# Seven products for more pairs of weight blocks, and two kinds of addition moved from VectorE to adding DMAs

## The chip, the cores and the metric

The kernel runs on one core of a Trainium2 chip. The metric is device time in microseconds: a median of runs, and beside it the time of one profiled execution, from which all rows of the trace come.

## What is computed

A causal decoder trunk of two layers on 256 tokens of width 2048, in float32. Each layer is a token mixer and then an MLP, each behind an RMSNorm, all added into one residual stream:

```python
h = rms_norm(x, mix_norm_g[i]);  x = x + mixer_i(h)        # layer 0: forgetting attention, layer 1: dilated windows
h = rms_norm(x, mlp_norm_g[i])
a = jax.nn.relu(h @ w_up)                                   # 2048 -> 8192
x = x + (a * a) @ w_down                                    # 8192 -> 2048
```

The two MLPs hold the change. In each, `w_up` is 2048 x 8192 and `w_down` is 8192 x 2048.

## The kernel before

**Units and pairs.** A matrix product is cut into units of 512 output columns. A unit walks over its contracted dimension in eight *pairs*: a pair is 256 rows by 512 columns of weights, 512 KB, loaded by SyncE's queue (SP) into a buffer `raw` (`loaded`, L335). Float32 precision is kept by splitting each operand into a high and a low part: ScalarE (ACT) casts `raw` to `hi` (`cut`, L342), VectorE (DVE) subtracts it to get `lo` (L348), and TensorE (PE) multiplies high by high, high by low and low by high.

**Three forms of a pair.** `whole` (L386 to L388) does two chunks of 128 rows, two halves of the tokens and three part products: 12 matmuls of 512 columns. `parts` (L413 to L438) treats the pair as a 2 x 2 block product and does it by seven block products and not eight: 7 x 3 = 21 matmuls of 256 columns. For that it needs sums of token blocks (`sigma`, made once per norm) and sums of weight blocks, made anew for each pair: one DVE addition of 512 columns (L413), two of 256 (L418, L420), and two cuts, one of 768 columns of the weights themselves and one of 1024 columns of the sums. It takes two buffers `raw` (one for the sums), two `hi` and two `lo`; a whole pair takes one of each. `quarters` (L407) is the whole form inside a unit that has `parts` pairs; its 12 matmuls go to the same banks of PSUM.

**The MLP.** It is done in four periods of 2048 hidden columns: `b` = 0 to 3. A period has four up units (`n` = 0 to 3) and, in the period after it, four down units that read their result. From period 1 on, up unit `n` is interleaved with down unit `n` of the period before, pair by pair, by the string `UU_D`; I call these 16 pairs a *round*. There are 12 rounds in each MLP, 24 in all. In period 0 only up units run: the first two share their pairs out as 6, 6, 2, 2, then the third, then the fourth. The table `HALVED[b][n]` says which pairs of an up unit go by `parts`: five of eight in all 24 up units of periods 1 to 3, none in period 0.

**The end of an up unit** (`up_end`): ACT copies four banks to SBUF (L968), DVE combines them by five additions (L973 to L986), ACT applies the ReLU (L991), DVE transposes in blocks (L994), four DMAs and one back take it through DRAM (`through_dram`), ACT squares (L1002) into a buffer `tr`, ACT casts the high part (L1007) and DVE subtracts the low part (L1009) into `aT`, which the down units read. The end of a down unit (`add_to_x`, L527) is one DVE addition of 1024 columns from PSUM into the residual stream.

**What sets the order.** All operations are entered in a plan (`Plan`) with an engine, an estimated time and the buffers they read and write. Buffers come in rings: an item waits until the former user of its slot is done. The plan is run through with the estimates, and the instructions are issued in the order of starts that comes out. The estimates (`on_act`, `on_dve`, `moved`, `gap`) thus shape only the order. Each engine works its own instructions strictly in this order, SP's queue of DMAs too: where the first waits for a buffer, those behind it wait as well. In the MLPs there are 7 `raw` (6 and one of the phase), 5 `hi`, 5 `lo`, and 4 `tr`.

Of the kernel before, what the change touches and what calls it, by code (L numbers as in the profile page):

```python
# [13 lines left out]
ALU = mybir.AluOpType  # L14
# [3 lines left out]
P = 128  # L18
D = 2048
S = 256  # L20
NT = S // P
NC = 512
# [13 lines left out]
PERIODS = DFF // D  # L36
# [52 lines left out]
class Plan:  # L89

    HANDOFF = 0.25
    LANDING = 2.1
    BACKLOG = 2.0
    FIRST = 14.0
# [40 lines left out]
    def gap(self, a, b):  # L137
        if a.eng == "dma":
            return self.LANDING
        if a.eng is None:  # L140
            return 0.0
        if a.eng == b.eng:
            return 0.0 if a.eng == "pe" else 0.06
        return self.HANDOFF

    def order(self, rounds=3):
        for ring in self.rings:
# [81 lines left out]
def trunk(ctx: ExitStack, tc, x, fox_w_in, fox_b_f, fox_q_gain, fox_k_gain, fox_w_out, dil_w_in,  # L229
          dil_q_gain, dil_k_gain, dil_w_out, mix_norm_g, mlp_norm_g, mlp_w_up, mlp_w_down, out):  # L230
    nc = tc.nc
    plan = Plan(["fox", "mlp0", "dil", "mlp1"])
    add = plan.add
    T = {}

    def v(item):
        return T[item.slot if isinstance(item, Item) else item]

    def r(item):
        return v(item).bitcast(F32R)  # L240
# [18 lines left out]
    N_RAW = 6  # L259
    N_HI = 4  # L260
    N_LO = 4
    N_Z = 1
    N_C = 1
    raw_ring = ring("raw", N_RAW, 2 * NC)
# [4 lines left out]
    blocks_ring = Ring(plan, [f"blocks{i}" for i in range(4)])  # L269
    rings = {}  # L270
    for ph in ("mlp0", "mlp1"):
        rings[ph] = dict(sigma=ring("sigma", 4, 2 * 4 * 2 * P, ph), tr=ring("tr", 4, NT * NC, ph),
                         z=ring("z", N_Z, 6 * S, ph), c=ring("c", N_C, NC, ph))
    for ph, n_sets, heads in (("fox", 1, 4), ("dil", 3, 2)):
        rings[ph] = dict(
            s=ring("s", 4, 3 * P, ph), w=ring("w", 4 if ph == "fox" else 3, NT * NC, ph),
# [3 lines left out]
            ph=ring("ph", 2, S, ph), pl=ring("pl", 2, S, ph), pw=ring("pw", 2, P, ph))  # L280
# [163 lines left out]
    def through_dram(turned, into, size=NT * NC):  # L444
        blocks = blocks_ring.take()
        for i in range(4):
            def go(i=i):
                nc.sync.dma_start(v(blocks)[:, :, :, i, :].rearrange("t j c x -> c t j x"),
                                  v(turned)[32 * i:32 * i + 32, 0:size].rearrange("p (t j x) -> p t j x", t=NT, j=4))
            add("dma", 0.45, go, reads=[turned], writes=[(blocks, i)])  # L450
# [24 lines left out]
    def x_keys(n):  # L475
        return [(f"x{n}", t) for t in range(NT)]
# [41 lines left out]
            reads=[room, (sigma, 0)], writes=[(sigma, 1)])  # L518


    def add_to_x(n, then=None):
        def end(banks):
            pair = banks[0].slot[0]

            def go():
                at = v(f"x{n}").rearrange("p (t h n) -> p t h n", t=NT, h=2)
                nc.vector.tensor_add(at, at, v(pair).rearrange("p (t n h) -> p t h n", t=NT, h=2))  # L527
# [413 lines left out]
    out_proj(oT, fox_w_out[0], then1)  # L941


    def up_end(l, phase, source, halved):
        own = rings[phase]

        def end(banks):
            z, turned = own["z"].take(), own["tr"].take()
# [51 lines left out]
            for t in range(NT):  # L1000
# [5 lines left out]
            source.items.append(a)  # L1006
            add("act", on_act(2 * NC), lambda: nc.scalar.copy(r(a)[:, 0:2 * NC], v(turned)), reads=[(turned, t) for t in range(NT)],  # L1007
                writes=[(a, b, 0) for b in range(4)])
            add("dve", on_dve(2 * NC), lambda: nc.vector.tensor_sub(r(a)[:, 2 * NC:], v(turned), v(a)[:, 0:2 * NC]),  # L1009
                reads=[*((turned, t) for t in range(NT)), *((a, b, 0) for b in range(4))], writes=[(a, b, 1) for b in range(4)])  # L1010
        return end

    AC, BE = ("A0", "A1", "C0", "C1"), ("B0", "B1")
    UU_D = "UUDUDUDUDUDUDUDD"

    def mlp(l, layer, phase, source, sigmas, then, last=None):
        for weights, name, n in ((raw_ring, "raw", MORE[0]), (hi_ring, "hi", MORE[1]), (lo_ring, "lo", MORE[2])):
            slots = [f"{phase}_{name}{i}" for i in range(n)]
            in_phase[phase].update({s: 2 * NC for s in slots})
            weights.more(slots, phase)  # L1020
        downs = []
        turn = 0
        for b in range(PERIODS):
            a = Source()
            ups = []
            for n in range(4):
                halved = HALVED[b][n]
                banks = AC if halved else ("A0", "A1") if b or n % 2 == 0 else ("B0", "B1")
                ups.append(Unit(source, mlp_w_up[layer], 0, [(b * D + n * NC, NC)], banks,
                                up_end(l, phase, a, halved), halved, sigmas))  # L1030
            if b == 0:
                paired(ups[0], ups[1])
                ups[2].blocks(NP)
                ups[3].blocks(NP)
            else:
                for u, d in zip(ups, downs):
                    for c in UU_D:
                        (u if c == "U" else d).block()
            downs = []
            for n in range(NX):  # L1040
                banks = ("E0", "E1") if turn % 2 == 0 else ("B0", "B1")
                turn += 1
                end = add_to_x(n, then if b == PERIODS - 1 else None)
# [217 lines left out]
```

## Time and profile before

| | |
|---|---|
| median of 3 runs | 2120.92 us (2120.85 to 2121.04) |
| profiled execution | 2121.22 us; its span from first to last instruction 2119.5 us |
| DVE, ACT, POOL busy | 1669.8, 1266.0, 57.8 us |
| HBM read, written | 455.26, 35.65 MB |
| the 12 rounds of the first MLP | 460.5 to 943.4 us after the span's start |
| the 12 rounds of the second MLP | 1549.0 to 2031.9 us |

A row of the table of groups reads: line, engine, operation, output<-inputs, shape, count, then busy time, mean duration of one in ns, then idle time of the engine just before them and what ended it. PE's matmuls overlap in the records, so their pace is read from the starts in the timeline and not from their durations.

### The profile page before, as it was taken

The page shows a single profiled execution, that of the slowest core. Times are in us where ns is not written, and L with a number is a line of the kernel's source. Part 1 is how long each engine was busy: PE and PEld are TensorE (multiplying, and loading weights), DVE is VectorE, ACT ScalarE, POOL GpSimd, SP SyncE. Part 2 cuts the span into 40 slices and gives each one's busy share as a digit, 9 for nine tenths or more (in the row PEclk, how much of TensorE's full clock was granted, in tenths as well). Part 3 has the DMA queues.
Part 4 walks back from the last instruction along what each step waited for, and adds up shares of the span by engine and source line. Part 5 has one row for each costly group of instructions (what it writes and reads, how often), then busy time and mean ns, then how long its engine had stood idle before and what let it go on. Part 6 is the DMA issues. An engine that isn't in the chain of part 4 may idle for free.

```text
span 2119.5 us, 30432 instructions
## 1 busy us (share of the span) xinstructions
PE 2109.8 (100%) x11285; PEld 1888.0 (89%) x11285; DVE 1669.8 (79%) x2092; ACT 1266.0 (60%) x1640; POOL 57.8 (3%) x51
## 2 busy tenths in 40 slices
PE   9999999999999999999999999999999999999999
PEld 7888888889999999998888888888899999999988
DVE  6777777678899899886787777777678898898874
ACT  5555556566666666666555555556666666666652
POOL 1011000000000000000010000000000000000000
PEclk9999999999999999999999999999999999999999
DMA  7777668777767777777786776768767777777773
GB/s 247 233 221 199 212 217 262 240 243 238 228 225 242 241 225 237 245 257 260 227 259 200 235 223 207 249 203 285 237 223 232 249 228 230 248 229 228 248 259 129
DMA packets 336133, 492.93 MB, mean 233 GB/s; under 512 B 21928, under 2 KB 137712, under 8 KB 335984
## 3 DMA queue, kind: packets, MB, share of 16 engines
q1 hardware_dynamic: 335712, 490.86, 72.9%
q8 instruction: 88, 1.44, 0.3%
q14 instruction: 61, 0.50, 0.1%
q10 hardware_dynamic: 272, 0.13, 0.0%
HBM read 455.26 MB, written 35.65 MB: 232 GB/s over the span
## 4 chain that ended last, share of the span: by engine, by line
PE 99%; DMA 0%; SPq 0%; DVE 0%; issue 0%; ACT 0%
PE bank_B L386 11%; PE bank_B L388 11%; PE bank_B L387 11%; PE bank_C L407 9%; PE bank_A L386 7%; PE bank_A L388 7%; PE bank_A L387 7%; PE bank_E L386 7%; PE bank_E L388 7%; PE bank_E L387 7%; PE bank_A L437 3%; PE bank_A L438 3%; PE bank_A L436 3%; PE bank_C L437 2%; PE bank_C L438 2%; PE bank_C L436 2%
## 5 line engine op out<-in xcount | busy, mean ns | idle before, releaser
L342 ACT CAST hi<-raw 128x1024 fp32r<-128x1024 f32 (+1 forms) x720 | 736.0, 1026 | 585.0 <-PE bank_B L388 171.1
L348 DVE TENSOR_TENSOR lo<-raw,hi 128x1024 fp32r<-128x1024 f32 (+1 forms) x720 | 854.7, 1193 | 277.1 <-ACT hi L342 261.7
L386 PE MATMUL bank_A<-hi,hT 128*128 128x512 f32 x552 | 212.0, 384 | 0.0
L388 PE MATMUL bank_A<-hi,hT 128*128 128x512 f32 x552 | 210.3, 381 | 0.0
L387 PE MATMUL bank_A<-lo,hT 128*128 128x512 f32 x552 | 210.2, 381 | 0.0
L386 PE MATMUL bank_B<-hi,aT 128*128 128x512 f32 x520 | 197.5, 380 | 0.5 <-ACT aT L646 0.5
L388 PE MATMUL bank_B<-hi,aT 128*128 128x512 f32 x520 | 197.1, 379 | 0.0
L387 PE MATMUL bank_B<-lo,aT 128*128 128x512 f32 x520 | 197.1, 379 | 0.0
L386 PE MATMUL bank_B<-hi,hT 128*128 128x512 f32 x480 | 183.7, 383 | 0.0
L387 PE MATMUL bank_B<-lo,hT 128*128 128x512 f32 x480 | 181.9, 379 | 0.0
L388 PE MATMUL bank_B<-hi,hT 128*128 128x512 f32 x480 | 181.9, 379 | 0.0
L386 PE MATMUL bank_E<-hi,aT 128*128 128x512 f32 x472 | 179.0, 379 | 0.0
L387 PE MATMUL bank_E<-lo,aT 128*128 128x512 f32 x472 | 178.9, 379 | 0.0
L388 PE MATMUL bank_E<-hi,aT 128*128 128x512 f32 x472 | 178.9, 379 | 0.0
L342 ACT CAST mlp_hi<-raw 128x1024 fp32r<-128x1024 f32 (+1 forms) x108 | 109.7, 1016 | 90.1 <-PE bank_E L388 27.0
L348 DVE TENSOR_TENSOR mlp_lo<-raw,mlp_hi 128x1024 fp32r<-128x1024 f32 (+1 forms) x108 | 127.0, 1176 | 27.7 <-ACT mlp_hi L342 24.1
L407 PE MATMUL bank_C<-hi,hT 128*128 128x512 f32 x430 | 138.5, 379 | 0.0
L388 PEld LDWEIGHTS bank_A<-hi,hT 128*128 128x128 f32 x552 | 104.9, 190 | 15.4 <-DVE hT L711 0.5
L386 PEld LDWEIGHTS bank_A<-hi,hT 128*128 128x128 f32 x552 | 105.1, 190 | 14.0
L387 PEld LDWEIGHTS bank_A<-lo,hT 128*128 128x128 f32 x552 | 105.0, 190 | 14.1
L388 PEld LDWEIGHTS bank_B<-hi,aT 128*128 128x128 f32 x520 | 98.3, 189 | 14.1 <-DVE aT L647 0.2
L386 PEld LDWEIGHTS bank_B<-hi,aT 128*128 128x128 f32 x520 | 98.4, 189 | 13.3 <-ACT aT L646 0.7
(360 smaller groups left out, 4391.7 us busy)
## 6 DMA issues: line engine op xcount, KB each, us to landing
raw<-in_mlp_w_up_dram SPq DMA_DIRECT2D x222, 512.0 KB, 4.5
raw<-in_mlp_w_down_dram SPq DMA_DIRECT2D x222, 512.0 KB, 4.8
raw<-in_fox_w_in_dram SPq DMA_DIRECT2D x96, 512.0 KB, 4.6
raw<-in_dil_w_in_dram SPq DMA_DIRECT2D x192, 256.0 KB, 3.1
blocks<-mlp_tr SPq DMA_DIRECT2D x176, 128.0 KB, 3.6
mlp_z<-blocks SPq DMA_DIRECT2D x44, 512.0 KB, 5.4
mlp_raw<-in_mlp_w_up_dram SPq DMA_DIRECT2D x34, 512.0 KB, 4.5
mlp_raw<-in_mlp_w_down_dram SPq DMA_DIRECT2D x34, 512.0 KB, 4.6
```

The source lines that it names most:

```text
L342: add("act", on_act(n), lambda: nc.scalar.copy(r(hi)[:, 0:n], v(src)[:, at:at + n]), reads=keys, writes=[hi])
L348: add("dve", on_dve(n), lambda: nc.vector.tensor_sub(r(lo)[:, 0:n], v(src)[:, at:at + n], v(hi)[:, 0:n]), reads=[*keys, hi], writes=[lo])
L386: nc.tensor.matmul(acc, a, h, start=first and i == 0, stop=False)
L387: nc.tensor.matmul(acc, a, l, start=False, stop=False)
L388: nc.tensor.matmul(acc, b, h, start=False, stop=last and i == 1)
L407: nc.tensor.matmul(to, m, w, start=False, stop=False)
L436: nc.tensor.matmul(acc, a(0), w(0, at), start=first and edge & 1 == 1, stop=False)
L437: nc.tensor.matmul(acc, a(0), w(1, at), start=False, stop=False)
L438: nc.tensor.matmul(acc, a(1), w(0, at), start=False, stop=last and edge & 2 == 2)
```

## The change

Up pairs by seven products go from 120 to 178: seven of eight in 23 of the 24 up units of periods 1 to 3, six in the other, and six of eight in the third up unit of period 0 of each MLP. The string of a round changes from `UUDUDUDUDUDUDUDD` to `UUUDDUUDDUUDUDDD`.

In periods 0 to 2 of each MLP the end of a down unit no longer adds on DVE: ACT copies its two banks into a new buffer `sums` (two copies of 512 columns) and a DMA issued by GpSimd (POOL) adds this into `x`; these are the 24 residual additions. For the first three up units of each period ACT writes, beside the high part, its negative into the low half of `aT`, and a DMA issued by POOL adds the full value `turned` to that, which leaves the low part; these are the 24 low parts (3 x 4 x 2). The fourth up unit of each period keeps the DVE subtraction.

Buffers: `tr` 4 to 3, one `sums` is new; the phase's own `raw`, `hi`, `lo` go from 1, 1, 1 to 0, 2, 1, so that there are 6, 6 and 5. Up units of period 0 that are not halved use `sums` in the place of `z`. The estimates of the plan change as well.

```diff
-MORE = (1, 1, 1)
-HALVED = [[(), (), (), ()], [FIVE] * 4, [FIVE] * 4, [FIVE] * 4]
+MORE = (0, 2, 1)
+BY_DMA = True
+LOW_BY_DMA = True
+HALVED = [[(), (), (0, 3, 4, 5, 6, 7), ()],
+          [(0, 1, 3, 4, 5, 6, 7), (0, 1, 3, 4, 5, 6, 7), (0, 1, 3, 4, 5, 6, 7), (0, 1, 3, 4, 5, 6, 7)],
+          [(0, 1, 3, 4, 5, 6, 7), (0, 1, 3, 4, 5, 6, 7), (0, 1, 3, 5, 6, 7), (0, 1, 3, 4, 5, 6, 7)],
+          [(0, 1, 3, 4, 5, 6, 7), (0, 1, 3, 4, 5, 6, 7), (0, 1, 3, 4, 5, 6, 7), (0, 1, 3, 4, 5, 6, 7)]]
 def on_act(n, accum=False):
-    return 0.24 + 0.00083 * n + (0.19 if accum else 0)
+    return 0.12 + 0.00083 * n + (0.19 if accum else 0)
 def on_dve(n, inputs=2):
-    return 0.17 + (0.00104 if inputs == 2 else 0.00054) * n
+    return 0.085 + (0.00104 if inputs == 2 else 0.00054) * n
 def moved(kb):
-    return kb / 380.0
+    return kb / 335.0
...
+    def added(to, of, reads, writes, us):
+        add("pool", 1.2, lambda: nc.gpsimd.dma_start(to(), of(), accum_op=ALU.add), reads=[*reads, *writes])
+        add("dma", us, None, reads=reads, writes=writes)
...
+            if room is not None:
+                sums = room.take()
+                for t in range(NT):
+                    def go(t=t):
+                        nc.scalar.copy(halves(v(sums)[:, t * NC:(t + 1) * NC], S), by_column(v(banks[t]), S))
+                    add("act", on_act(NC), go, reads=[banks[t]], writes=[(sums, t)])
+                added(lambda: v(f"x{n}"), lambda: v(sums), [(sums, t) for t in range(NT)], x_keys(n), 2.55)
+                return
...
-            add("dve", on_dve(2 * NC), lambda: nc.vector.tensor_sub(r(a)[:, 2 * NC:], v(turned), v(a)[:, 0:2 * NC]),
...
+            if by_dma:
+                add("act", on_act(2 * NC), lambda: nc.scalar.mul(r(a)[:, 2 * NC:], v(turned), -1.0), reads=whole, writes=low)
+                added(lambda: v(a)[:, 2 * NC:], lambda: v(turned), whole, low, 2.55)
...
-    UU_D = "UUDUDUDUDUDUDUDD"
+    UU_D = "UUUDDUUDDUUDUDDD"
```

More of the change, by code (lines that the diff above doesn't have):

```diff
@@ L142, in gap @@
         if a.eng == b.eng:
-            return 0.0 if a.eng == "pe" else 0.06
-        return self.HANDOFF
+            return 0.0 if a.eng == "pe" else 0.12
+        return 0.3 if a.eng == "pe" else self.HANDOFF
     def order(self, rounds=3):
@@ L261, in trunk @@
     N_LO = 4
+    N_TR = 3
     N_Z = 1
@@ L271, in trunk @@
     for ph in ("mlp0", "mlp1"):
[L272 to L273 removed]
+        rings[ph] = dict(sigma=ring("sigma", 4, 2 * 4 * 2 * P, ph), tr=ring("tr", N_TR, NT * NC, ph),
+                         z=ring("z", N_Z, 6 * S, ph), c=ring("c", N_C, NC, ph), sums=ring("sums", 1, NT * NC, ph))
     for ph, n_sets, heads in (("fox", 1, 4), ("dil", 3, 2)):
@@ L941, in trunk, with up_end @@
     out_proj(oT, fox_w_out[0], then1)
-    def up_end(l, phase, source, halved):
+    def up_end(l, phase, source, halved, by_dma, room):
         own = rings[phase]
         def end(banks):
-            z, turned = own["z"].take(), own["tr"].take()
+            z, turned = own[room].take(), own["tr"].take()
             by = lambda t: v(f"rstd{l}")[:, t:t + 1]
@@ L1008, in end @@
                 writes=[(a, b, 0) for b in range(4)])
-            add("dve", on_dve(2 * NC), lambda: nc.vector.tensor_sub(r(a)[:, 2 * NC:], v(turned), v(a)[:, 0:2 * NC]),
-                reads=[*((turned, t) for t in range(NT)), *((a, b, 0) for b in range(4))], writes=[(a, b, 1) for b in range(4)])
-        return end
-    AC, BE = ("A0", "A1", "C0", "C1"), ("B0", "B1")
-    UU_D = "UUDUDUDUDUDUDUDD"
+            whole = [(turned, t) for t in range(NT)]
+            low = [(a, b, 1) for b in range(4)]
+            if by_dma:
+                add("act", on_act(2 * NC), lambda: nc.scalar.mul(r(a)[:, 2 * NC:], v(turned), -1.0), reads=whole, writes=low)
+                added(lambda: v(a)[:, 2 * NC:], lambda: v(turned), whole, low, 2.55)
+            else:
+                add("dve", on_dve(2 * NC), lambda: nc.vector.tensor_sub(r(a)[:, 2 * NC:], v(turned), v(a)[:, 0:2 * NC]),
+                    reads=[*whole, *((a, b, 0) for b in range(4))], writes=low)
+        return end
+    AC, BE = ("A0", "A1", "C0", "C1"), ("B0", "B1", "E0", "E1")
+    UU_D = "UUUDDUUDDUUDUDDD"
     def mlp(l, layer, phase, source, sigmas, then, last=None):
@@ L1027, in mlp @@
                 halved = HALVED[b][n]
-                banks = AC if halved else ("A0", "A1") if b or n % 2 == 0 else ("B0", "B1")
+                banks = (AC if halved else AC[:2]) if b or n % 2 == 0 else BE if halved else BE[:2]
                 ups.append(Unit(source, mlp_w_up[layer], 0, [(b * D + n * NC, NC)], banks,
-                                up_end(l, phase, a, halved), halved, sigmas))
+                                up_end(l, phase, a, halved, LOW_BY_DMA and n < 3, "z" if b or halved else "sums"), halved, sigmas))
             if b == 0:
@@ L1042, in mlp @@
                 turn += 1
-                end = add_to_x(n, then if b == PERIODS - 1 else None)
+                end = add_to_x(n, then) if b == PERIODS - 1 else add_to_x(n, None, rings[phase]["sums"] if BY_DMA else None)
                 downs.append(Unit(a, mlp_w_down[layer], b * D, [(n * NC, NC)], banks, end, adding=ADDING if b < PERIODS - 1 else ()))
```

6 lines of the change are left out of this document (3 added, 3 removed).

## The prediction

> **What bounds the kernel now.** I read the page first (busy times, clock, the chain that ended last), then PE's waits, PE's timeline, and then, for the rounds alone, the busy times of a window and the waits of DVE.
>
> ```profile
> PE 2109.8 (100%) x11285; PEld 1888.0 (89%) x11285; DVE 1669.8 (79%) x2092; ACT 1266.0 (60%) x1640; POOL 57.8 (3%) x51
> PE 99%; DMA 0%; SPq 0%; DVE 0%; issue 0%; ACT 0%
> PEclk9999999999999999999999999999999999999999
> ```
>
> PE is the bound: the chain of work that ended last lies on it for 99% of the span, at the full granted clock. A busy PE alone would prove little, so I looked for its waits:
>
> ```profile
> PE bank_E L701 <- DMA x<-in_x_dram: 2.1, 2, 1.7
> PE bank_C L659 <- POOL ident masks.py:199: 1.7, 1, 1.7
> PE bank_E L670 <- DMA fox_s<-in_mix_norm_g_dram: 1.3, 1, 1.3
> PE bank_B L1191 <- DVE x L1206: 0.8, 1, 0.8
> PE bank_B L386 <- ACT aT L646: 0.5, 1, 0.5
> ```
>
> That is the whole list (what for, what ended it, total us, times, longest): 6.4 us, at the start, at the end and once before an output projection, nothing in the MLPs. So PE time saved in the rounds comes off the total, as long as nothing else grows past PE there. How much time a pair takes is read from the starts:
>
> ```profile
> 601.13 0.38 PE L386 MATMUL bank_B<-hi,aT 128*128 128x512 f32 x1
> 603.72 0.27 PE L436 MATMUL bank_A<-hi,hT 128*128 128x256 f32 x1
> 606.07 0.38 PE L386 MATMUL bank_B<-hi,aT 128*128 128x512 f32 x1
> ```
>
> From 601.13 to 603.72 lie the 12 matmuls of a whole pair, 2.59 us; from 603.72 to 606.07 the 21 of a pair by seven products, 2.35 us. The rounds of the first MLP check this:
>
> ```profile
> 460.50:943.40 482.90, 482.90 (x2859) 440.73 (x2858) 425.93 (x518) 309.34 (x361) 0.00 (x0) 1.00 0.74 237
> ```
>
> (Window, its length, then busy us of PE, weight loads, DVE, ACT, POOL with their counts; clock, DMA share, GB/s.) A round lasts 482.9 / 12 = 40.24 us. It has 5 pairs of the short form and 11 of the long one; with 2.592 for the long one (12 x 0.216) the short one is (40.24 - 28.51) / 5 = 2.346. The gain per pair is 0.246 us.
>
> **The change: PE.** 58 pairs more (46 in the rounds, 6 in period 0 of each MLP) x 0.246 = 14.3 us. Two more units are split into two forms, which costs nothing in columns. A new round lasts 40.24 - 14.3 x 46 / 58 / 24 = 39.77 us on PE alone.
>
> **DVE.** Here is the price. The rows by shape, and starts that follow one another:
>
> ```profile
> L348 DVE TENSOR_TENSOR lo<-raw,hi 128x1024 fp32r<-128x1024 f32 x642 | 780.8, 1222 | 260.8 <-ACT hi L342 245.7 <-DMA mlp_z<-blocks 2.7 <-DMA raw<-in_mlp_w_down_dram 2.0
> L348 DVE TENSOR_TENSOR lo<-raw,hi 128x768 fp32r<-128x768 f32 x78 | 74.4, 954 | 16.4 <-ACT hi L342 16.0
> L413 DVE TENSOR_TENSOR raw<-raw 128x512 f32<-128x512 f32 x72 | 49.6, 689 | 32.7 <-DMA raw<-in_mlp_w_up_dram 32.3
> L418 DVE TENSOR_TENSOR raw<-raw,raw 128x256 f32<-128x256 f32 x72 | 30.2, 419 | 0.6
> L1009 DVE TENSOR_TENSOR aT<-mlp_tr,aT 128x1024 fp32r<-128x1024 f32 x32 | 39.0, 1217 | 7.6 <-ACT aT L1007 7.3
> L527 DVE TENSOR_TENSOR x<-x,bank_B 128x1024 f32<-128x1024 f32 x19 | 23.1, 1217 | 2.9 <-PE bank_B L388 2.9
> L994 DVE STREAM_TRANSPOSE mlp_tr<-mlp_z 128x1024 f32<-128x1024 f32 x32 | 39.6, 1239 | 3.9 <-ACT mlp_z L953 3.3 <-ACT mlp_z L991 0.7
> L973 DVE TENSOR_TENSOR mlp_z<-mlp_z,mlp_c 128x512 f32<-128x512 f32 x24 | 16.4, 684 | 0.3 <-ACT mlp_z L968 0.3
> L974 DVE TENSOR_TENSOR mlp_z<-mlp_z 128x256 f32<-128x256 f32 x24 | 10.2, 425 | 0.8
> ```
>
> ```profile
> 652.44 0.69 DVE L413 TENSOR_TENSOR raw<-raw 128x512 f32<-128x512 f32 x1
> 653.04 1.22 DVE L348 TENSOR_TENSOR lo<-raw,hi 128x1024 fp32r<-128x1024 f32 x1
> 654.18 0.41 DVE L418 TENSOR_TENSOR raw<-raw,raw 128x256 f32<-128x256 f32 x1
> ...
> 655.12 0.96 DVE L348 TENSOR_TENSOR lo<-raw,hi 128x768 fp32r<-128x768 f32 x1 [0.53 <-ACT hi L342]
> 656.00 0.42 DVE L420 TENSOR_TENSOR raw<-raw,raw 128x256 f32<-128x256 f32 x1
> 656.34 0.69 DVE L413 TENSOR_TENSOR raw<-raw 128x512 f32<-128x512 f32 x1
> ```
>
> The reader should compare length and distance: the 1024-column subtraction lasts 1.22 us, but the next instruction starts 1.14 after it; 0.69 becomes 0.60, 0.96 becomes 0.88, 0.42 becomes 0.34. About 0.08 us of each overlaps with the next where nothing is waited for. So a halved pair adds to DVE's work 0.60 + 2 x 0.34 + 0.88 = 2.16 us (it takes 3.3, a whole one 1.14).
>
> DVE's busy time per round is 425.93 / 12 = 35.5 us of 40.24. New: + 2 x 2.16 (seven for five) - 1.14 (L527, every round) - 0.75 x 1.14 (L1009, three rounds of four) = 37.8 us of 39.77, 95% in place of 88%. DVE stays below PE, with 1.95 us a round to spare. Without the two moves to the DMAs it would be 39.8, no room at all.
>
> Is the room usable? DVE idles 4.7 us a round now. Its waits from 500 to 900 us (ten rounds):
>
> ```profile
> DVE lo L348 <- ACT hi L342: 20.0, 32, 0.9
> DVE raw L413 <- DMA raw<-in_mlp_w_up_dram: 14.2, 15, 1.5
> ACT hi L342 <- PE bank_E L388: 27.3, 22, 1.8
> ```
>
> The larger one is back pressure: ACT's cast waits for PE to give a `hi` back, so DVE is held because it is ahead. The 1.4 us a round for a load are real. I followed one new round by hand with five `lo`: DVE's excess over PE is 3.3 - 2.35 = 0.95 us for each halved pair, and it gains 1.45 on each whole one. The string never has more than two halved pairs in a row before a whole one (index 2 is whole), and three down pairs (7.8 us of PE, 3.4 of DVE) lie where the end of the up unit falls (three additions like L973, two like L974 and the transpose: 4.1 us on DVE). The tightest point is the second up pair of a round, ready some 1.7 us before PE needs it. I take no stall in the rounds.
>
> Period 0 is less even: five halved pairs in a row want 5 x 0.95 = 4.8 us from the lead that five `lo` allow, about 5 us, and the transpose of the unit before falls among them. I take 0.5 us in each MLP, 1 in all; bounds 0 and 2.5 each.
>
> **ACT** has 309.34 / 12 = 25.8 us a round. It gains two casts of 768 columns, two copies of a bank and 0.75 of a cast of 1024:
>
> ```profile
> L342 ACT CAST hi<-raw 128x768 fp32r<-128x768 f32 x78 | 65.2, 836 | 69.6 <-PE bank_E L388 27.0 <-PE bank_B L388 15.3 <-PE bank_C L407 13.8
> L968 ACT COPY mlp_z<-bank_A 128x512 f32<-128x512 f32 x24 | 14.2, 590 | 0.0
> L1007 ACT CAST aT<-mlp_tr 128x1024 fp32r<-128x1024 f32 x32 | 33.7, 1053 | 16.0 <-PE bank_B L387 15.7
> ```
>
> 2 x 0.84 + 2 x 0.59 + 0.75 x 1.05 = 3.6: 29.4 us of 39.77. Nothing.
>
> **The adding DMAs.** No run here shows one. The nearest rows:
>
> ```profile
> q1 hardware_dynamic: 335712, 490.86, 72.9%
> raw<-in_mlp_w_up_dram SPq DMA_DIRECT2D x222, 512.0 KB, 4.5
> mlp_z<-blocks SPq DMA_DIRECT2D x44, 512.0 KB, 5.4
> ```
>
> A plain 512 KB occupies the queues 0.524 x 0.729 x 2119.5 / 490.86 = 1.65 us; one that adds must read both operands, so 1.65 to 3.3, and I take 2.5 between them. With 1.75 a round the DMA share goes from 0.74 to about 0.85. They land after perhaps 5 to 8 us, bounded below by the 4.5 of a load. The Trainium skill (DMA: Bandwidth & Descriptors, Anatomy of one DMA) fits a DMA issued by GpSimd with 2.0 us plus the bytes over 436 GB/s, by which the estimate would be 3.2 us. Nobody waits soon: the next addition to the same `x` comes four rounds later, `sums` is used again a round later, and `aT` of the first three units is read a round or more later (the fourth, which is read first after its end, stays on DVE). POOL does nothing in this window (0.00 above), so its wait in front of a DMA holds up no one.
>
> What they can do is delay loads. A load is issued when the slot six places back is free:
>
> ```profile
> SPq L335 <- DVE lo L348: 129.5, 75, 4.1
> ```
>
> SP already waits for slots, and the ring falls from 7 to 6 while a round takes 23 places in place of 21: a load is issued 4.2 pairs ahead (10.4 us), not 5.3 (13.5). It lands in 4.5, and the pair before it must also be worked off; some 3 us remain. An adding DMA in front takes up to 2.5 of them. No cost, but this is the first cover to go.
>
> **Sum.** 2121.2 (profiled execution; 0.3 above the median, 1.7 above its span) - 14.3 + 1.0 = 2107.9; I say 2108.
>
> **Rivals.**
> *Slower: DVE becomes the bound of the rounds.* It decides when DVE needs 1.95 us a round more than my 37.8, that is, when the 0.08 us of overlap is lost for 24 of its 49 instructions (518 / 12 + 8 - 1.75). With fewer idle stretches but more instructions that wait for ACT or their own forerunner this can happen. Lost for three in four it is 40.7 us, 24 x 0.95 = 23 us over PE: 2131; for all, 41.7 and 2154. Against it: the window counts busy time as it is, with the overlaps that the present order already loses. The Trainium skill bears on this from two sides: VectorE: DVE Perf Modes, The DRAIN you can't avoid, has the next operation wait until the pipe is empty (unless it is not held), which taken strictly gives the 2154; Perfetto Trace Analysis, Optimizing Scalar/DVE Operations, lets half of the fixed part overlap with the next instruction. The starts above, 1.14 apart at 1.22 long, agree with the second.
> *Loads come late.* With six slots and the adding DMAs in between, DVE's 1.4 us a round of waits for loads grows by some 1.5, and little slack is left: I price a loss of 0.3 us a round on PE, 7 us, 2115 (2110 to 2117).
> *Nothing gained.* Late loads and period 0 together take 10 to 18 us: 2117 to 2125. That the change does not do what it says is excluded by the table: its rows hold 6, 28, 27 and 28, twice 89 is 178.
>
> **Chances.** Forecast (2105 to 2110) 0.60; late loads 0.17; nothing gained 0.08; DVE the bound 0.15. A measurement tells about 0.2% (4.2 us) from no change, so faster means below 2116.7: 0.77; same 0.08; slower 0.15. The range goes from 2105 (no stall, 0.26 a pair: 15.1 us, and 1 us for the reading of the starts) to 2120, a third into the case of nothing gained; the rest of that and the DVE case are left out, 0.2.
>
> **What would show it.** Right: L436 to L438 with 178 x 7 = 1246 each, still 0.11 us apart; DVE near 37.8 of 39.8 us in a round; L527 with 15 instructions in place of 39, L1009 with 8; DMA share about 0.85; PE's waits still without an entry in the MLPs. Wrong: PE waits on DVE `lo` L348 in the rounds (DVE's case, if DVE has no idle time; late loads, if L413 waits long for `raw`), or in the third unit of period 0; adding DMAs that take far over 8 us to land and hold `aT` or `tr`.

## The result and the profile after

The changed kernel takes 2134.72 us (median of 4 runs, 2133.38 to 2135.88), the kernel before 2120.98 on the same chip: a ratio of 1.0063 [1.0046, 1.008]. It is slower by 13.7 us where I forecast 12.9 us faster (2108 against 2120.92). The profiled execution took 2134.26 us, its span 2132.5. (A slip in my description: seven of eight pairs go by `parts` in 22 of the 24 up units and six in two, one in each MLP; the 178 pairs are right.)

Line numbers move: cuts L348 and L354, loads L341, `whole` L392 to L394, `parts` L442 to L444, its additions L419, L424, L426, the adding DMA L529, `add_to_x` L546, `through_dram` L454 and L459, the transpose L1013.

The page of the kernel after: busy times, queues (packets, MB, share of the queues' time), the chain that ended last, one group, and DMA issues (KB each, median us from issue to landing).

```profile
PE 2106.1 (99%) x11809; PEld 1894.8 (89%) x11809; DVE 1735.7 (81%) x2286; ACT 1343.2 (63%) x1778; POOL 105.0 (5%) x99
...
q1 hardware_dynamic: 335712, 490.86, 70.7%
q0 software_dynamic: 6912, 25.17, 6.4%
...
PE 72%; DMA 11%; DVE 10%; issue 4%; ACT 2%; SPq 1%; POOL 0%; DVEq 0%; ACTq 0%
...
L419 DVE TENSOR_TENSOR raw<-raw 128x512 f32<-128x512 f32 x178 | 121.9, 688 | 67.7 <-DMA raw<-in_mlp_w_up_dram 67.0
...
raw<-in_mlp_w_up_dram SPq DMA_DIRECT2D x256, 512.0 KB, 4.9
...
blocks<-mlp_tr SPq DMA_DIRECT2D x176, 128.0 KB, 4.9
```

The chain no longer lies on PE for 99% but for 72%; the rest is loads and DVE. L419 with 178 instructions shows that the change does what it says. Its idle time before them is 67.7 us, for loads (before: 32.7). The adding DMAs in the view of issues, and one of the groups that they empty (it had 32 instructions before):

```profile
aT<-mlp_tr POOLq DMA_DIRECT2D x24, 512.0 KB, 7.3
x<-mlp_sums POOLq DMA_DIRECT2D x24, 512.0 KB, 7.4
```

```profile
L1034 DVE TENSOR_TENSOR aT<-mlp_tr,aT 128x1024 fp32r<-128x1024 f32 x8 | 9.8, 1222 | 4.5 <-ACT aT L1026 4.5
```

The 12 rounds of each MLP, from the first matmul of the first round to the first one behind the last (busy us of PE, weight loads, DVE, ACT, POOL; clock, DMA share, GB/s):

```profile
461.12:947.49 486.37, 482.01 (x3065) 444.32 (x3063) 448.67 (x591) 339.36 (x416) 18.05 (x21) 1.00 0.83 258
1552.71:2044.35 491.64, 482.80 (x3065) 443.37 (x3064) 448.69 (x591) 339.31 (x417) 18.05 (x21) 1.00 0.82 255
```

A round takes 40.53 and 40.97 us, and should take 39.77. DVE is busy 37.4 us a round, near the 37.8 that I reckoned: it isn't full. But PE now waits in the MLPs, where before it never did (first rows of PE's waits in the whole run):

```profile
PE bank_A L443 <- DVE lo L354: 4.2, 10, 0.9
PE bank_A L443 <- DVE mlp_lo L354: 2.7, 3, 2.1
PE bank_B L393 <- DVE lo L354: 2.7, 4, 1.3
...
PE bank_C L413 <- DVE lo L354: 1.8, 3, 0.9
```

These waits show only a part. I added up, over the trace, what the starts of successive matmuls in the two MLPs lie further apart than 0.216 us (512 columns) and 0.112 (256). Before it is 0; after it is 23.9 us: 16.1 in 22 single losses of over 0.35 us and 7.8 in smaller ones. I call this sum PE's loss. All of it lies in the rounds, 9.4 us in the first MLP and 14.6 in the second; period 0 lost nothing. It closes the account: 2121.2 - 14.3 (the saving of PE) + 23.9 = 2130.8, and the stages outside the MLPs are 2.9 us longer: 2133.7, against 2134.26.

DVE's waits in the rounds of the first MLP, after and then before:

```profile
DVE raw L419 <- DMA raw<-in_mlp_w_up_dram: 28.2, 30, 2.7
DVE lo L354 <- ACT hi L348: 3.0, 6, 1.2
DVE lo L354 <- ACT mlp_hi L348: 2.4, 4, 1.2
```

```profile
DVE lo L348 <- ACT hi L342: 25.0, 40, 1.1
DVE raw L413 <- DMA raw<-in_mlp_w_up_dram: 15.9, 16, 1.8
DVE mlp_lo L348 <- ACT mlp_hi L342: 6.4, 9, 1.0
DVE raw L413 <- DMA mlp_raw<-in_mlp_w_up_dram: 2.2, 1, 2.2
...
DVE mlp_raw L413 <- DMA raw<-in_mlp_w_up_dram: 0.9, 2, 0.5
```

The reader should see two things swap. The wait for ACT, which was back pressure (DVE was ahead of PE and held), is nearly gone; the wait for loads has grown from 19.0 to 28.2 us (83 pairs by seven products wait here in place of 60). DVE has hardly any lead any more, so a late load reaches PE. No wait in this trace is ended by the landing of an adding DMA, so it isn't a buffer held by one that PE or DVE lacks. The largest case, in the timelines of SP, DVE and PE, and the clock in stretches around it:

```profile
559.49 0.37 SPq L459 DMA_DIRECT2D mlp_z<-blocks  x1
559.95 0.42 SPq L341 DMA_DIRECT2D raw<-in_mlp_w_up_dram  x1
564.40 5.68 SPq L341 DMA_DIRECT2D raw<-in_mlp_w_down_dram  x3
```

```profile
567.40 0.69 DVE L419 TENSOR_TENSOR raw<-raw 128x512 f32<-128x512 f32 x1 [2.69 <-DMA raw<-in_mlp_w_up_dram]
568.12 0.42 DVE L424 TENSOR_TENSOR raw<-raw,raw 128x256 f32<-128x256 f32 x1
568.47 1.22 DVE L354 TENSOR_TENSOR mlp_lo<-raw,hi 128x1024 fp32r<-128x1024 f32 x1
```

```profile
567.39 0.28 PE L442 MATMUL bank_A<-hi,mlp_sigma 128*128 128x256 f32 x1
569.74 0.49 PE L443 MATMUL bank_A<-mlp_lo,mlp_sigma 128*128 128x256 f32 x1 [2.07 <-DVE mlp_lo L354]
570.02 0.42 PE L444 MATMUL bank_A<-hi,mlp_sigma 128*128 128x256 f32 x1
570.24 0.42 PE L442 MATMUL bank_A<-hi,mlp_sigma 128*128 128x256 f32 x1
```

```profile
562.00:567.30 5.30, 5.30 (x41) 5.03 (x40) 2.71 (x4) 3.99 (x5) 0.00 (x0) 1.00 0.63 214
567.40:569.70 2.30, 0.27 (x3) 0.08 (x1) 2.27 (x4) 1.70 (x2) 0.00 (x0) 1.00 0.67 257
569.75:573.20 3.45, 3.45 (x14) 3.27 (x15) 3.45 (x5) 2.12 (x3) 0.00 (x0) 0.52 0.62 197
```

The load issued at 559.95, right behind the way back L459, ends DVE's wait at 567.4, some 7.4 us later. DVE idles 2.69 us, PE's next low part is late, and PE stands 2.07 us. Then its matmuls of 256 columns follow one another at 0.21 us and not at 0.11, at a granted clock of 0.52, for 3.4 us: 1.7 us more are lost after the wait has ended. No adding DMA flies beside this load: the last one was issued at 547.11 us and landed 7.3 us later. A late load has more than one cause.

### The profile page after: what moved, and what is told of

Its sections match the earlier page's. It is cut to its first block, busy times and chain, and to the rows that moved or that the text cites. A ratio compares the mean times of both kernels' runs of the same rounds, so it can differ in the third digit from the quotient of the medians.

```text
span 2132.5 us, 32383 instructions
## 1 busy us (share of the span) xinstructions
PE 2106.1 (99%) x11809; PEld 1894.8 (89%) x11809; DVE 1735.7 (81%) x2286; ACT 1343.2 (63%) x1778; POOL 105.0 (5%) x99
## 3 DMA queue, kind: packets, MB, share of 16 engines
q0 software_dynamic: 6912, 25.17, 6.4%
## 4 chain that ended last, share of the span: by engine, by line
PE 72%; DMA 11%; DVE 10%; issue 4%; ACT 2%; SPq 1%; POOL 0%; DVEq 0%; ACTq 0%
DMA raw<-in_mlp_w_up_dram 9%; PE bank_B L392 8%; PE bank_B L393 8%; PE bank_B L394 8%; DVE lo L354 5%; PE bank_E L393 5%; PE bank_E L392 5%; PE bank_E L394 5%; PE bank_A L392 5%; PE bank_A L393 5%; PE bank_A L394 5%; PE bank_A L443 2%; PE bank_A L444 2%; PE bank_A L442 2%; PE bank_C L413 1%
## 5 line engine op out<-in xcount | busy, mean ns | idle before, releaser
L348 ACT CAST hi<-raw 128x1024 fp32r<-128x1024 f32 (+1 forms) x746 | 744.0, 1013 | 547.6 <-PE bank_B L394 123.5
L354 DVE TENSOR_TENSOR lo<-raw,hi 128x1024 fp32r<-128x1024 f32 (+1 forms) x654 | 767.9, 1183 | 191.4 <-ACT hi L348 150.2
L348 ACT CAST mlp_hi<-raw 128x1024 fp32r<-128x1024 f32 (+1 forms) x232 | 227.8, 997 | 123.1 <-DVE raw L426 45.9
L354 DVE TENSOR_TENSOR lo<-raw,mlp_hi 128x1024 fp32r<-128x1024 f32 (+1 forms) x186 | 211.7, 1146 | 20.1 <-ACT mlp_hi L348 9.2
L392 PE MATMUL bank_A<-hi,hT 128*128 128x512 f32 x480 | 184.7, 385 | 0.0
L394 PE MATMUL bank_A<-hi,hT 128*128 128x512 f32 x480 | 182.4, 380 | 0.0
L392 PE MATMUL bank_B<-hi,hT 128*128 128x512 f32 x464 | 177.7, 383 | 0.0
L419 DVE TENSOR_TENSOR raw<-raw 128x512 f32<-128x512 f32 x178 | 121.9, 688 | 67.7 <-DMA raw<-in_mlp_w_up_dram 67.0
L394 PE MATMUL bank_B<-hi,hT 128*128 128x512 f32 x464 | 175.9, 379 | 0.0
L392 PE MATMUL bank_B<-hi,aT 128*128 128x512 f32 x452 | 171.6, 380 | 0.0
L394 PE MATMUL bank_B<-hi,aT 128*128 128x512 f32 x452 | 171.3, 379 | 0.0
L392 PE MATMUL bank_E<-hi,aT 128*128 128x512 f32 x408 | 155.0, 380 | 0.0
L394 PE MATMUL bank_E<-hi,aT 128*128 128x512 f32 x408 | 154.8, 379 | 0.0
L443 PE MATMUL bank_A<-lo,mlp_sigma 128*128 128x256 f32 x444 | 123.7, 279 | 4.4 <-DVE lo L354 4.0
L354 DVE TENSOR_TENSOR mlp_lo<-raw,hi 128x1024 fp32r<-128x1024 f32 (+1 forms) x92 | 104.1, 1131 | 10.3 <-PE bank_E L393 4.1
L393 PEld LDWEIGHTS bank_B<-lo,aT 128*128 128x128 f32 x508 | 96.1, 189 | 16.6 <-DVE lo L354 3.9
L394 PEld LDWEIGHTS bank_A<-hi,hT 128*128 128x128 f32 x480 | 91.0, 190 | 13.0
```

Of the source, the lines that this page charges most:

```text
L348: add("act", on_act(n), lambda: nc.scalar.copy(r(hi)[:, 0:n], v(src)[:, at:at + n]), reads=keys, writes=[hi])
L354: add("dve", on_dve(n), lambda: nc.vector.tensor_sub(r(lo)[:, 0:n], v(src)[:, at:at + n], v(hi)[:, 0:n]), reads=[*keys, hi], writes=[lo])
L392: nc.tensor.matmul(acc, a, h, start=first and i == 0, stop=False)
L393: nc.tensor.matmul(acc, a, l, start=False, stop=False)
L394: nc.tensor.matmul(acc, b, h, start=False, stop=last and i == 1)
L419: add("dve", on_dve(2 * q), lambda: nc.vector.tensor_add(v(sums)[:, 0:2 * q].rearrange("p (g n) -> p g n", g=2), v(raw)[:, q:3 * q].rearra ...
```

## The experiments

Each kernel is timed against the kernel before on the same chip (2120.5 to 2121.1). The theories: **traffic** (the adding DMAs make loads land late, and DVE has no lead to absorb it); **room** (DVE has too little time left in a round); **ring** (six `raw` in place of seven); **queue** (loads stand behind the way through DRAM in SP's queue); **order** (the estimates put instructions elsewhere). PE's loss is the sum explained above; it is that of the profiled execution alone, which can lie some us off the median.

| run | median, us | ratio | PE's loss, us |
|---|---|---|---|
| after | 2134.72 | 1.0063 [1.0046, 1.008] | 23.9 |
| e1_no_dma_adds | 2145.34 | 1.0115 [1.0099, 1.0132] | 37.5 |
| e2_seven_raw | 2166.98 | 1.0218 [1.0203, 1.0233] | 54.2 |
| e3_adds_only | 2132.13 | 1.0055 [1.004, 1.007] | 7.1 |
| e4_order_only | 2130.84 | 1.0048 [1.0033, 1.0063] | 0.5 |
| e5_old_order | 2205.95 | 1.04 [1.0379, 1.0422] | 96.8 |
| e6_adds_old_order | 2141.61 | 1.01 [1.0083, 1.0117] | 20.4 |
| e7_six_of_eight | 2158.36 | 1.0181 [1.0166, 1.0196] | 42.3 |
| e8_six_adds_x | 2146.34 | 1.0124 [1.0109, 1.0139] | 32.5 |
| e9_small_adds | 2116.13 | 0.9974 [0.9956, 0.9991] | 7.5 |
| e10_short_ends | 2123.28 | 1.0009 [0.9998, 1.0019] | 15.2 |
| e11_both | 2109.88 | 0.9947 [0.9932, 0.9962] | 0 |
| e12_turn_on_pool | 2201.57 | 1.0368 [1.0339, 1.0397] | 57.8 |
| e13_in_four | 2132.43 | 1.0061 [1.0044, 1.0078] | 19.9 |
| e14_plain | 2126.78 | 1.0022 [1.0013, 1.0031] | 13.9 |
| e15_small_x | 2134.45 | 1.0064 [1.0048, 1.0081] | 27.3 |
| e16_turn_on_act | 2158.96 | 1.0181 [1.0166, 1.0197] | 37.5 |
| e17_small_low | 2122.01 | 1.0001 [0.9992, 1.001] | 13.4 |
| e18_low_on_dve | 2139.87 | 1.0087 [1.0073, 1.0101] | 31.1 |

**The parts of the change alone, and the order.** First the two moves undone (e1), seven `raw` (e2), the moves without the pairs (e3), the order without anything else (e4).

```diff
-BY_DMA = True
-LOW_BY_DMA = True
+BY_DMA = False
+LOW_BY_DMA = False
```

> The changed kernel with both kinds of adding DMA taken back: 178 pairs by seven products, all additions on DVE. Theory L (the adding DMAs make the loads late, and DVE's waits for raw at L419 starve PE): loads land in about 4.5 us again, the waits of L419 fall from 30 us in twelve rounds to 16 or less, and the time falls to 2118-2128, though DVE has 39.0 us of work in a round of 39.8. Theory D (DVE is simply too full, and the DMAs helped it): DVE has 2 us a round more, PE loses most of that, 24 x 1.5 = 36 us more: 2150-2175, with DVE without idle time.

```diff
-MORE = (0, 2, 1)
+MORE = (1, 1, 1)
```

> The changed kernel with 7 raw, 5 hi and 5 lo in place of 6, 6 and 5; nothing else. Theory R (the look-ahead of the loads fell with the ring from 7 to 6): a load is issued 2.5 us earlier, which covers most of the lateness; L419's waits halve, time 2115-2125. Theory L without R: the seventh slot does not help because SP's queue itself is held up (behind the block transfers); 2130-2137. Theory D: no change, 2132-2138.

```diff
-HALVED = [[(), (), (0, 3, 4, 5, 6, 7), ()],
...
+HALVED = [[(), (), (), ()], [FIVE] * 4, [FIVE] * 4, [FIVE] * 4]
-MORE = (0, 2, 1)
+MORE = (1, 1, 1)
-    UU_D = "UUUDDUUDDUUDUDDD"
+    UU_D = "UUDUDUDUDUDUDUDD"
```

> The changed kernel with the old table (120 pairs by seven products), the old string and 7 raw, 5 hi, 5 lo; the adding DMAs and the new order stay. PE's own time is that of before. Theory L in its strong form (adding DMAs alone starve PE): 2126-2135, PE waits in the rounds. Theory L with DVE's slack as the cover: DVE has 33.5 us of 40.2 a round and absorbs late loads: 2119-2123, loads beside adding DMAs still land 1 to 2 us later. Theory D: 2119-2122.

e4 is the kernel before with the changed estimates (`on_act`, `on_dve`, `moved`, and those of `gap`) and nothing else.

> The kernel before with the new estimates of the plan alone: same operations, other order. Theory O (part of the loss, some 3 us outside the MLPs, comes from the new order): 2123-2125, with the first matmuls later. Otherwise 2120-2122.

Measured: 2145.34, 2166.98, 2132.13 and 2130.84 us. In e1 DVE's waits for loads in the rounds of the first MLP fall from 28.2 us to 17.2, as the traffic theory has it. Yet without the moves the kernel is 10.6 us slower than with them, and PE's waits for DVE grow, in the whole run of e1:

```profile
PE bank_A L443 <- DVE lo L354: 13.8, 15, 1.3
```

This speaks for the relief of DVE: the moves seem to cost something and still to earn more. The planner's order differs between the two kernels, so the 10.6 us are not the price of the moves alone. A seventh `raw` at the price of a `hi` is worse by 32 us; the order changes with it, so the ring is not refuted, only not supported. The order is a cost by itself: with 120 pairs and no adding DMA, 9.9 us in the median. Of the 6.4 us by which the profiled execution is longer, PE's loss explains 0.5; the stages ahead of the MLPs take the rest, 1.5 us ahead of the first and 4.3 between the two. The moves with the new estimates and 120 pairs (e3) cost 7.1 us of PE's loss, though the time is only 1.3 us above that of e4.

**The old estimates.** e5 is the changed kernel with the old estimates, e6 the kernel before with the two moves and the old estimates, e7 the kernel before with six pairs of eight (144), e8 is e7 with the residual additions by DMA. e3, e6 and e8 are made from the changed kernel and keep its three `tr`, where e7 and the kernel before have four.

```diff
-    return 0.12 + 0.00083 * n + (0.19 if accum else 0)
+    return 0.24 + 0.00083 * n + (0.19 if accum else 0)
...
-    return kb / 335.0
+    return kb / 380.0
```

> The changed kernel with the old estimates of the plan: 178 pairs, adding DMAs, 6 raw; the order alone is another. Theory O (the order that the new estimates give costs some 10 us, in the attention stages and in the rounds, as it did at 120 pairs): 2118-2127, the stages outside the MLPs back at their old length. Theory L (the rounds lose 24 us to late loads whatever the order, only the attention stages lose to the order): 2127-2133. If the new estimates are what the fuller rounds need: 2140 or more, lost in the rounds.

> 120 pairs, the old string, 7 raw, the old estimates, and the adding DMAs: the kernel before with the two moves alone. Theory O: 2119-2123, as before, since the loss of the run with the adds and the new order was that of the order. Theory L in its strong form: 2125-2132, with the rounds 3 us longer in each MLP.

```diff
-FIVE = (0, 2, 4, 5, 7)
+FIVE = (0, 1, 3, 4, 6, 7)
```

> The kernel before with six of eight pairs by seven products (0, 1, 3, 4, 6, 7), so 144; no adding DMA, old estimates, old string, 7 raw. PE's own time is 24 x 0.246 = 5.9 us shorter; DVE has 37.6 us in a round of 40.0. If DVE at 94% is what PE cannot bear (theory D): 2122-2135. If loads and order are what hurt (L, O): 2114-2118.

> The same 144 pairs, old estimates, old string, 7 raw, with the residual additions (24) by adding DMAs and the low parts on DVE. DVE has 36.5 us in a round of 40.0. Theory D: better than without the DMAs, 2114-2118. Theory L: worse than without them by 3 us or more.

Measured: 2205.95, 2141.61, 2158.36, 2146.34 us. The new estimates are worth 71 us to the changed kernel; they are no ornament of it. And with the old ones every step of the change loses: the two moves 20.6 us, six pairs of eight 37 us in place of a gain of 5.9 (24 pairs x 0.246), of which the residual additions by DMA give 12 back. In e7 the first rows of PE's waits name the end of the up unit:

```profile
PE bank_E L386 <- ACT aT L1007: 11.5, 4, 3.6
PE bank_A L437 <- DVE lo L348: 6.7, 8, 1.5
```

With more short pairs ahead of it on ACT and DVE, the up unit's result comes too late for the down unit. In e6 DVE waits for ACT as long as before (26.1 us in the rounds of the first MLP, 25.0 before), and yet PE loses: single waits of DVE for a load reach 4.6 us there, against 2.2 before. A lead can cover only a delay that is shorter than it. These four tell of an order that doesn't fit, and can't price the adding DMAs, nor the fourth `tr`. For that the order has to stay. All kernels from here on but the last keep the order of the changed kernel's instructions on PE, DVE and ACT.

**Traffic and room, in the same order.** e9 moves 64 of 1024 columns in each adding DMA, so most of each addition is left out. e10 cuts the five additions at the end of an up unit to two of 8 columns, so its combination is mostly left out; this also ends the up unit earlier, and not only DVE's work. e11 does both.

```diff
-nc.gpsimd.dma_start(to(), of(), accum_op=ALU.add)
+nc.gpsimd.dma_start(to()[:, 0:64], of()[:, 0:64], accum_op=ALU.add)
```

> The changed kernel, instruction for instruction in its own order, but each adding DMA moves 64 of 1024 columns (most of each addition is left out), so that it costs the queues next to nothing. Theory L (adding DMAs make the loads late): loads land in 4.5 to 5.2 us, L419's waits in the rounds fall from 60 us to 30 or less, and the time to 2110-2120. Theory D (DVE too full whatever the loads): 2130-2135.

```diff
 def first_two():
-    nc.vector.tensor_add(zq()[:, 1:5:3, :], zq()[:, 1:5:3, :], c2()[:, 0:1, :].to_broadcast([P, 2, S]))
...
+    nc.vector.tensor_add(zq()[:, 1, 0:8], zq()[:, 1, 0:8], c2()[:, 0, 0:8])
```

> The changed kernel in its own order, with the five additions at the end of an up unit cut to two of 8 columns (most of the combination of the seven products is left out): DVE has some 2.5 us a round less. The adding DMAs are whole. Theory D: the rounds lose almost nothing, 2108-2115. Theory L: late loads still starve PE, 2125-2133.

> Both of these at once, same order. If late loads and DVE's fullness are all there is, PE has no waits in the rounds: 2108-2111 (2107 from PE's own time, and the 1 to 3 us that the new order loses outside the MLPs). If 2115 or more remains, the order or the ring of six raw costs by itself.

Measured: 2116.13, 2123.28 and 2109.88 us. Against the changed kernel the traffic is worth 18.6 us, DVE's room 11.4, both 24.8: less than the sum of 30.0, for either one gives back part of the other's loss. In e11 PE's loss is 0, a round takes 39.75 us where I had reckoned 39.77, and the time is within 2 us of my forecast. So neither the ring of six `raw` nor this order costs PE anything in the rounds by itself. Its DVE waits in the rounds of the first MLP:

```profile
DVE raw L419 <- DMA raw<-in_mlp_w_up_dram: 14.3, 14, 2.3
DVE lo L354 <- issue: 14.1, 13, 1.3
...
DVE lo L354 <- PE bank_E L393: 3.7, 4, 1.5
```

The wait for loads has halved, and waits of `lo` that no load ends are back, some of them for PE itself: DVE is ahead again. The same view in e9, and then in e10, where the traffic is whole:

```profile
DVE raw L419 <- DMA raw<-in_mlp_w_up_dram: 16.8, 16, 2.8
```

```profile
DVE raw L419 <- DMA raw<-in_mlp_w_up_dram: 42.0, 45, 3.0
```

In e10 the wait for loads is longer than the 28.2 us of the changed kernel, and yet PE loses less. I read this so: a wait for a load costs what is left of it when DVE's lead is used up. No run shows the lead by itself.

**Another queue for the way through DRAM.** e12 issues the DMAs of `through_dram` from POOL's queue, e16 from ACT's.

```diff
-                nc.sync.dma_start(v(blocks)[:, :, :, i, :].rearrange("t j c x -> c t j x"),
+                nc.gpsimd.dma_start(v(blocks)[:, :, :, i, :].rearrange("t j c x -> c t j x"),
...
-            nc.sync.dma_start(v(into)[:, 0:size].rearrange("p (t y) -> p t y", t=NT),
+            nc.gpsimd.dma_start(v(into)[:, 0:size].rearrange("p (t y) -> p t y", t=NT),
```

> The changed kernel, complete, with the way through DRAM (four block transfers and one back) issued from POOL's queue and not from SP's, so that no load waits behind them on SP. Theory Q (loads are late because SP's queue stands behind the transposes and the landing of the blocks, some 35 us in twelve rounds): 2112-2122. Theory L (the transfers themselves crowd the loads): 2130-2136, or worse if POOL's own queue holds up the transfers.

> The DMAs that take the transposed blocks through DRAM are issued from ACT's queue and no longer from SP's. On SP they stood in front of loads (SP waited 16.7 us in one stretch of 12 rounds for the way back). Queue theory (loads are late because they are issued late, behind the way back): loads go out earlier, the 28 to 32 us of DVE's waits for loads in 12 rounds fall by a third, 2125 to 2130. Traffic theory: the loads land late whenever they are issued; what SP waited, ACT now waits in front of its casts, 2140 or more, with waits of ACT for blocks and of PE for lo or hi.

Measured: 2201.57 and 2158.96 us, 67 and 24 slower than with SP. The way through DRAM serves the other stages too, and about half of the loss lies there: the first MLP begins at 396.4 and 386.1 us in place of 379.7, and the stretch between the MLPs is 20 and 7 us longer. The rest is more loss on PE in the MLPs. The wait isn't gone, it has moved. One row of POOL's waits in e12, and one of ACT's in e16:

```profile
POOL blocks L454 <- DVE mlp_tr L1013: 175.6, 26, 28.6
```

```profile
ACT hi L348 <- DMA blocks<-mlp_tr: 18.8, 6, 4.8
```

On POOL the adding DMAs stand behind it, on ACT the casts of later weights. So the queue theory is not supported; that loads would be on time with a queue for themselves alone could not be tried without a new wait elsewhere.

**What in the adding DMAs costs.** e13 issues each in four pieces of 256 columns; in e14 they are plain copies, so the additions are left out; in e15 only the residual additions are cut to 64 columns, in e17 only the low parts (the rest of these additions is left out).

```diff
-nc.gpsimd.dma_start(to(), of(), accum_op=ALU.add)
+[nc.gpsimd.dma_start(to()[:, i:i + 256], of()[:, i:i + 256], accum_op=ALU.add) for i in range(0, 1024, 256)]
```

> Each adding DMA is issued as four DMAs of 256 of the 1024 columns, back to back from POOL's queue; nothing else changes, the order of every engine's instructions is that of the changed kernel. An issue took POOL 0.86 us, so the 2.84 us of queue time now spread over some 3.5 us. Burst theory (a load loses because it lands beside one large burst): a load meets a quarter of the burst at a time, half of the 18.6 us that the traffic cost comes back, 2125 (2120 to 2129). Total theory (the queues' time counts, however it is cut): 2134.7 within 3 us, with the time of POOL's queue unchanged at about 2.84 us for each 512 KB. Rival: smaller rows cost more each, queue time rises above 3.2 us for each 512 KB, 2138 or more.

```diff
-nc.gpsimd.dma_start(to(), of(), accum_op=ALU.add)
+nc.gpsimd.dma_start(to(), of())
```

> The adding DMAs become plain copies of the same size (the 24 residual additions and 24 low parts are replaced by an overwrite, so part of the computation is left out); the order of instructions is that of the changed kernel. If adding costs because both operands are read, POOL's queue shows about 1.65 us for each 512 KB, as for a load, in place of 2.84, and of the 18.6 us that the adding DMAs' traffic cost about 1.2/2.8 comes back, some 8: 2127 (2123 to 2130). If the adding itself is free and only the bytes written count, the queue time stays near 2.84 and the time at 2134.7.

```diff
-nc.gpsimd.dma_start(to(), of(), accum_op=ALU.add)
+nc.gpsimd.dma_start(to()[:, 0:n], of()[:, 0:n], accum_op=ALU.add)
```

In e15 `n` is 64 for the residual additions and 1024 for the low parts, in e17 the other way round.

> Only the 24 residual additions move 64 of 1024 columns (the rest of each is left out); the 24 low parts stay whole. The order is that of the changed kernel. If the cost goes by traffic, half of the 18.6 us goes: 2125.4 (2122 to 2128). If the low parts carry it (they fall together with the DMAs that transpose, at the end of an up unit): 2131 or more. If the residual additions carry it: 2120 or less.

> The mirror of the run with small residual additions: the 24 low parts move 64 of 1024 columns (the rest of each is left out), the 24 residual additions are whole; same order. With the residual additions small the time was 2134.5, no gain. If the low parts carry the cost of the traffic: 2117 (2115 to 2120). If either kind alone is enough to fill up what little room there is (the two don't add, only the last one removed pays): 2130 or more.

Measured: 2132.43, 2126.78, 2134.45 and 2122.01 us. The queue that POOL feeds, in e13 and then in e14 (after: 25.17 MB, 6.4%):

```profile
q0 software_dynamic: 27648, 25.18, 7.8%
```

```profile
q0 software_dynamic: 6912, 25.17, 3.1%
```

Per DMA of 512 KB the changed kernel shows 0.064 x 2132.5 / 48 = 2.84 us of the queues' time, a plain copy 0.031 x 2121.9 / 48 = 1.37, pieces with rows of a quarter of the length 3.46. Adding doubles the cost, and taking that away gives 7.9 us back, as the traffic theory expected (8; the ten runs of e14 lie between 2121.85 and 2130.31). Pieces change nothing that can be told apart, though each addition takes more of the queues: a burst as such is not the cause, and the time in the queues by itself is not the price. And the two kinds are far from equal: the low parts alone are worth 12.7 us, the residual additions alone 0.3 and 6 once the low parts are gone (2122.01 to 2116.13). The way back through DRAM shows that the residual additions do slow something. SP's wait for it in the rounds of the first MLP, in e15 and in e17 (after: 16.7, 15, 2.5):

```profile
SPq L459 <- DMA blocks<-mlp_tr: 6.2, 8, 1.6
```

```profile
SPq L459 <- DMA blocks<-mlp_tr: 16.0, 13, 2.9
```

The residual additions hold up the transposing DMAs (SP's wait falls from 16.7 to 6.2 us when they are small), and that alone costs nothing. The low parts' DMAs start anywhere from 0.3 to 29 us into a round, and one at 40, the residual additions all at 5.4 to 8.3 us. Of the loads in the rounds whose landing the trace tells, those that fly beside a low part's DMA and no other land after 6.27 us in the median (30 loads) in the changed kernel and after 5.04 (25) where the low parts are small, against 4.46 (84) with nothing beside them. Beside a residual addition alone 16 loads fall in two groups, ten at 3.5 to 4.6 us and six at 6.9 to 8.2. In 11 of PE's 22 larger losses, 6.5 us of 16.1, the last long wait of DVE for a load ahead of it was for one beside a low part's DMA. Why delays at these places reach PE and the others hardly do stays open: no run moved a low part's DMA to another place in the round without changing the rest.

**The kernel that would follow.** e18 has the low parts back on DVE and the residual additions by DMA; the order changes with it.

```diff
-LOW_BY_DMA = True
+LOW_BY_DMA = False
```

> A complete kernel: the change with the low parts back on DVE, the residual additions by DMA. The planner's order changes with it. If the low parts' DMAs carry the cost: the 18 us that went with the traffic come back, and DVE gets 0.75 x 1.14 = 0.86 us a round more, some 5 us lost: 2120 to 2125. If DVE's fullness counts as much as the traffic: 2130 to 2145, as with both on DVE (2145.3), and more PE waits on DVE lo.

Measured: 2139.87 us, 5.2 slower than the changed kernel, with 31.1 us of PE's loss. Either DVE's part of 0.86 us a round costs more than the 12.7 us that the traffic of the low parts took, or the other order does; the two are not told apart. No complete kernel that I tried beats the one before.

## Why the prediction was wrong, point by point

- **PE's saving, 14.3 us: right.** In e11, where PE never stands, the time is 11.1 us below before; with the 2.9 us outside the MLPs that the changed kernel shows, this is 14.0. Its rounds take 39.75 us.
- **"I take no stall in the rounds": the step that failed.** PE's loss in the rounds is 23.9 us where I had none; period 0, for which I had 1.0, lost nothing. I compared busy times and averages: 37.8 of 39.77 us on DVE, 3 us of slack for a load. DVE's held (37.4 us). But I had shown that DVE was held by back pressure, 2 us a round, and took that for idle time; as I read e9 to e11, it was the lead with which late loads were absorbed. The round that I followed by hand left 1.7 us at its tightest point and had every load on time; single waits for a load reach 2.7 us in the first MLP and 3.7 in the second. The change spends this lead and makes the loads later in the same step, and I priced the two apart.
- **"No cost, but this is the first cover to go": the cover went.** I took 2.5 us of the queues' time for an adding DMA, it is 2.84; 5 to 8 us to land, it is 7.3; a DMA share of 0.85, it is 0.83. The sizes were near. What failed was the conclusion: with the traffic of these DMAs nearly taken away the time falls by 18.6 us (e9). The Trainium skill (DMA: Bandwidth & Descriptors, Issuing engines are not separate DMA queues) says that DMAs issued by different engines run on the same 16 DMA engines and interleave. The trace agrees for the low parts: loads of SP's queue land after 4.46 us with nothing beside them and after 6.27 beside a low part's DMA of POOL's queue. Beside a residual addition alone ten of 16 loads lose nothing.
- **The rival "Loads come late"** named the right mechanism and the right row (L413, now L419, waits for `raw`). Its price of 7 us was too small by a factor of three, since I let it act alone, with DVE's lead untouched.
- **The rival "DVE becomes the bound"** had its sign and came near its price (2131), but by luck, since its mechanism is not there: DVE was to be full through lost overlap, and it idles 3 us a round. Its lack of room does count for up to 11.4 us (e10, which also ends the up unit earlier), and I read it as a lack of lead.
- **What follows a wait.** The sum had no term for it. The 22 larger losses are 16.1 us, 7.8 more go in small ones, 1.7 of them at half the clock after the longest wait.
- **The order.** I took the estimates to "shape only the order" and gave no cost to it. With 120 pairs they cost 9.9 us by themselves (e4); the changed kernel is 2.9 us longer outside the MLPs, and 2.7 of this stay in e11, where the adding DMAs are small; without them it would stand at 2205.95 (e5).
- **ACT, "Nothing": right as far as the waits go.** It is busy 339.36 / 12 = 28.3 us a round (I had 29.4), and no row of PE's waits in the rounds names it.

## What to carry to other kernels

Idle time that comes from back pressure is not room to fill: it can be the lead that hides late loads, so price a fuller feeding engine and later transfers together, from the wait that the lead hides and not from busy shares. Work that is moved to DMAs can stay on the path when loads share their engines: here it cost 18.6 us. Price it by the delay of the loads that are needed soonest; its queue time alone did not tell it. To price one part of a change where a planner lays out the instructions, keep the order and make the part small, since a kernel with the part taken out is another order.

## What the runs showed of the hardware

- A DMA that adds 512 KB within SBUF takes 2.84 us of the 16 queues' time against 1.37 for a plain copy of the same size, and lands 7.3 to 7.4 us after its issue; in rows of 1 KB and not 4 KB it takes 3.46 us for the same bytes. POOL's issue of one takes 0.86 us.
- After a wait of 2.07 us PE ran at a granted clock of 0.52 for 3.4 us. The Trainium skill (TensorE: Matmul & The Clock Gate, Part 1: The HAM clock gate) has the clock fall to half after an idle window of about 3.4 us and rise again after as long a busy one. The trace agrees with the second; the fall came here after less idle time, 2.35 us between starts, and did not come after another gap of 1.7 us at 1700.5. In other runs it came after 1.63 us between starts (e1 at 696.2) and did not after 2.42 (e6 at 623.5).
